# Every second gate and up block with four pairs of k-tiles in seven products, every down block of four strips with three, low parts in one piece, and small inputs later

## The chip, the cores and the metric

The kernel runs on one core of one Trainium2 chip. The metric is the device time of one execution in microseconds (us); the times given are medians of several runs. The core has a matrix engine (TensorE, in the profile PE for its matmuls and PEld for its weight loads), a vector engine (VectorE, DVE), a scalar engine (ScalarE, ACT), a general engine (GpSimd, POOL) and a queue engine (SyncE, SP) that here only issues DMAs. Each engine works through its own instructions in a fixed order and waits on semaphores for the others.

## The reference

Two layers of a decoder over 256 positions and 2048 features, in float32. What the change touches most is the feed-forward network (FFN) at the end of each layer:

```python
def swiglu(x, w_gate, w_up, w_down):
    return (jax.nn.silu(x @ w_gate) * (x @ w_up)) @ w_down
...
for layer in range(DEPTH):
    xn = rms_norm(x, norm_mix[layer])
    if layer % 2 == 0:
        x = x + mixer_mlstm_ssd(xn, *mixer_params[layer])
    else:
        x = x + mixer_moba(xn, *mixer_params[layer])
    x = x + swiglu(rms_norm(x, norm_ffn[layer]), *ffn_params[layer])
return rms_norm(x, final_norm)
```

`w_gate` and `w_up` are 2048 x 5632, `w_down` is 5632 x 2048. The mixer of layer 0 begins with a projection `xn @ w_in`, whose first columns are the queries of an mLSTM; its gates, a decay table and masks come from small inputs (`ssd_a_log`, `mlstm_gate_bias`, convolution weights and the like).

## The kernel before

**Matmuls in two parts.** A float32 operand is split into a high part of type fp32r (`wh`, `xh`: a copy by ACT) and the rest (`wl`, `xl`: source minus high part, by DVE). One product of a 128x128 tile of activations with 512 weight columns is then three matmuls that accumulate in PSUM: high by high, high by low, low by high (`add`, L473).

**Pairs of k-tiles.** `block` (L458) computes 256 positions by 1024 output columns (two strips of 512) over `nk` k-tiles, two k-tiles at a time. For each pair `weights` (L429) loads 2 x 512 KB of weights into `raw`, ACT writes `wh`, DVE writes `wl`. A **plain pair** ("P" in a plan) is 2 position halves x 2 strips x 2 k-tiles = 8 products, 24 matmuls. A **seven-product pair** ("S") follows Strassen's scheme: DVE forms four sums of weights from `raw` (L450, L451, L453) and needs four sums of activations (`sums_of`, `activation_sums`, kept in tiles `skx` or `skh`), both are split again, and 7 products, 21 matmuls, do. Its weight tiles come in two units: `wl<-raw` with 1536 elements (three parts) and `wl<-sums` with 2 x 1024. Products 2, 3, 4 go into the block's accumulators (`acc_f`, PSUM banks 0 to 3), products 1, 7, 5, 6 into `acc_e`, banks 4 to 7. When the last S pair is done, four additions by DVE make `pre` from `acc_e` (L521 to L525); when the last pair is done, two more, L1008 (or L909 for a down block), add `acc_f` to it. `acc_f` has one set of banks, so the next block's first matmul waits for the first of these two.

**Plans.** A plan says which kind comes at each position: `PLAN_X = "PSPSPSPP"` for gate and up blocks, `PLAN_LATE = "PPPSPSPP"` for the first of a network, `PLAN_H` for down blocks.

**The FFN** (`ffn`, L1001) goes through 11 strips of 512 hidden features in groups of 4, 4 and 3. `hidden` makes one strip: a block with the gate columns as one strip and the up columns as the other, then silu and product (`h`), a copy by a DMA of POOL's queue into `hr` (type fp32r), and eight transposes on PE into `p_tr` (banks 6, 7, 4, 5 in turn) that are split into `ha` or `hb`. They are put off by `later(wait, ...)`; while a block has S pairs left, `held` stops the clock of these waits. After a group, `add_blocks` runs two down blocks over its strips, the first for output columns 0 to 1023, the second for the others. I number strips 0 to 10 and call the two down blocks of a group its **first** and **second down block**.

**Buffers.** `raw` has three buffers and a spare that serves every fourth use; `wh` and `wl` have three each (`unit`, L122). A plain pair takes one of each, an S pair two. A buffer of `wh` is free when PE's last matmul with it is done.

**Order.** A scheduler places the instructions of each engine by priorities (`high_priority`) and by its own idea of when operands are ready, so the order on an engine, PE included, can differ from that of the code.

**The beginning.** PE runs eleven idle matmuls (`keep_busy`), while `first_x`, the first weights and small inputs are loaded: `alog`, `ident_in`, `pv`, `d_bc`, `gbias`, `mask_sl` on POOL's queue, `cw_rows` on ACT's. `chunks` (L352) brings the weights of a strip in pieces of two k-tiles, `input_ready` splits the input's k-tiles beside them.

## Time and profile before

| | |
|---|---|
| median of 3 runs | 2559.82 us (2558.21 to 2562.22) |
| the profiled execution | 2558.07 us, of which 2556.3 us are the span of its instructions |
| busy PE, DVE, ACT | 99%, 85%, 57% of the span |
| granted PE clock | 0.999 |
| FFN of layer 0 | blocks start at 769.65 us, end at 1469.77 us |
| FFN of layer 1 | blocks start at 1849.01 us |

The page gives one execution: busy time of each engine, the chain of work that ended last, and the costliest groups of instructions, each named by source line, engine, operation and tile, with idle time in front of them and who ended it. A matmul's row shows its start and about 0.39 us; the next one starts well before that has passed, so the distance from start to start is the one to count with.

### The profile page before, as it was taken

Reading aid. Unit: us, or ns where it says so; the run is one execution under the profiler, and the core shown is the slowest. Engines: PE = TensorE matmul, PEld = TensorE weight load, DVE = VectorE, ACT = ScalarE, POOL = GpSimd, SP = SyncE. Lnnn points to the kernel's source line nnn. Section 1 sums busy time; section 2 is a strip of 40 time slices with the busy share of each in tenths; the row PEclk is TensorE's granted clock in tenths of the full one; section 3 lists DMA queues with packets and bytes.
Section 4 is the critical chain, followed back from the end, with each engine's and each line's share of the span. In section 5 each row is a group of like instructions: output and inputs, shape, how many; then the busy total and the mean of one; then the engine's idle time right before and its main releaser. Section 6 shows DMA issues by size and latency. Waiting matters only on the chain.

```text
span 2556.3 us, 32504 instructions
## 1 busy us (share of the span) xinstructions
PE 2541.2 (99%) x12179; PEld 2129.6 (83%) x12179; DVE 2176.5 (85%) x2679; ACT 1465.2 (57%) x1940; POOL 59.7 (2%) x112
## 2 busy tenths in 40 slices
PE   9999999999999999999999999999999999999998
PEld 8888888888888888888888888888888888888887
DVE  5776778798989998999899987767999988998898
ACT  6465665566556554555455655666665545564554
POOL 1000010000000000000000000000000000000000
PEclk9999999999999999999999999999999999999999
DMA  8665576566565666566656556554556756575754
GB/s 281 181 209 185 165 231 185 167 204 214 181 214 182 217 212 202 200 222 216 196 200 212 196 172 230 165 165 149 196 184 213 234 177 222 198 239 167 236 190 165
DMA packets 257774, 509.58 MB, mean 199 GB/s; under 512 B 16232, under 2 KB 16512, under 8 KB 257104
## 3 DMA queue, kind: packets, MB, share of 16 engines
q1 hardware_dynamic: 249952, 483.20, 58.0%
q0 software_dynamic: 6224, 21.56, 2.4%
q10 hardware_dynamic: 1440, 2.75, 0.3%
q8 instruction: 95, 1.56, 0.2%
q14 instruction: 63, 0.52, 0.1%
HBM read 494.76 MB, written 2.14 MB: 194 GB/s over the span
## 4 chain that ended last, share of the span: by engine, by line
PE 94%; DVE 3%; issue 1%; DMA 1%; ACT 1%; SPq 0%; POOLq 0%; POOL 0%; DVEq 0%; ACTq 0%
PE acc_f L475 19%; PE acc_f L476 18%; PE acc_f L477 18%; PE acc_w L383 11%; PE acc_w L387 6%; PE acc_e L475 4%; PE acc_e L477 4%; PE acc_e L476 4%; PE acc_a L413 2%; PE acc_a L414 2%; PE acc_a L415 2%; PE p_y L872 1%; PE p_tr L284 1%; DVE wl L443 1%; DMA raw<-in_l_w_o 1%
## 5 line engine op out<-in xcount | busy, mean ns | idle before, releaser
L441 ACT CAST wh<-raw 128x1024 fp32r<-128x1024 f32 (+1 forms) x573 | 628.6, 1137 | 496.7 <-PE acc_f L477 384.1
L443 DVE TENSOR_TENSOR wl<-raw,wh 128x1024 fp32r<-128x1024 f32 (+1 forms) x573 | 745.8, 1327 | 119.2 <-ACT wh L441 115.8
L475 PE MATMUL acc_f<-wh,x 128*128 128x512 f32 x1122 | 438.6, 391 | 0.5 <-DVE xres L909 0.5
L477 PE MATMUL acc_f<-wh,x 128*128 128x512 f32 x1122 | 436.9, 389 | 0.0
L476 PE MATMUL acc_f<-wl,x 128*128 128x512 f32 x1122 | 436.6, 389 | 0.0
L368 DVE TENSOR_TENSOR wl<-raw,wh 128x1024 fp32r<-128x1024 f32 (+1 forms) x225 | 271.0, 1217 | 130.5 <-ACT wh L367 126.8
L441 ACT CAST wh<-sums 128x1024 fp32r<-128x1024 f32 x230 | 234.8, 1051 | 199.7 <-PE acc_f L477 137.4
L367 ACT CAST wh<-raw 128x1024 fp32r<-128x1024 f32 (+1 forms) x225 | 231.7, 1044 | 184.4 <-PE acc_w L383 94.4
L443 DVE TENSOR_TENSOR wl<-sums,wh 128x1024 fp32r<-128x1024 f32 x230 | 273.6, 1219 | 11.9 <-ACT wh L441 11.7
L477 PEld LDWEIGHTS acc_f<-wh,x 128*128 128x128 f32 x1122 | 210.6, 188 | 44.1
L475 PEld LDWEIGHTS acc_f<-wh,x 128*128 128x128 f32 x1122 | 210.6, 188 | 43.8 <-issue 0.9
L476 PEld LDWEIGHTS acc_f<-wl,x 128*128 128x128 f32 x1122 | 210.6, 188 | 43.0
L383 PE MATMUL acc_w<-xa,wh 128*128 128x512 f32 x768 | 207.9, 398 | 2.9 <-ACT wh L367 1.9
L383 PEld LDWEIGHTS acc_w<-xa,wh 128*128 128x128 f32 x768 | 139.2, 189 | 29.1 <-ACT wh L367 3.3
L450 DVE TENSOR_TENSOR sums<-raw 128x1024 f32<-128x1024 f32 x115 | 140.2, 1219 | 23.0 <-DMA raw<-in_l_ffn_up 11.3
L383 PE MATMUL acc_w<-x,wh 128*128 128x512 f32 x512 | 139.2, 399 | 0.0
L387 PE MATMUL acc_w<-xa,wl 128*128 128x256 f32 x768 | 121.1, 282 | 0.0
L387 PEld LDWEIGHTS acc_w<-xa,wl 128*128 128x128 f32 x768 | 109.6, 190 | 6.5
L383 PEld LDWEIGHTS acc_w<-x,wh 128*128 128x128 f32 x512 | 92.4, 189 | 16.9
L475 PE MATMUL acc_f<-wh,hb 128*128 128x512 f32 (+1 forms) x272 | 105.1, 387 | 0.0
L477 PE MATMUL acc_f<-wh,hb 128*128 128x512 f32 (+1 forms) x272 | 105.1, 386 | 0.0
L476 PE MATMUL acc_f<-wl,hb 128*128 128x512 f32 (+1 forms) x272 | 105.1, 386 | 0.0
(354 smaller groups left out, 4567.9 us busy)
## 6 DMA issues: line engine op xcount, KB each, us to landing
raw<-in_l_w_in SPq DMA_DIRECT2D x191, 512.0 KB, 3.7
raw<-in_l_ffn_gate SPq DMA_DIRECT2D x176, 512.0 KB, 3.9
raw<-in_l_ffn_up SPq DMA_DIRECT2D x176, 512.0 KB, 4.8
raw<-in_l_ffn_down SPq DMA_DIRECT2D x176, 512.0 KB, 5.1
raw<-in_l_w_qkv SPq DMA_DIRECT2D x96, 512.0 KB, 4.6
raw<-in_l_w_out SPq DMA_DIRECT2D x64, 512.0 KB, 5.1
raw<-in_l_w_o SPq DMA_DIRECT2D x32, 512.0 KB, 4.7
hr<-h POOLq DMA_DIRECT2D x40, 256.0 KB, 4.0
```

The lines of the kernel that those rows point to most:

```text
L367: nc.scalar.copy(wh[:, ks, :], raw[:, ks, :])
L368: nc.vector.tensor_sub(wl[:, ks, :], raw[:, ks, :], wh[:, ks, :].bitcast(F32))
L383: return nc.tensor.matmul(banks[f], wh[:, kk, f * P:(f + 1) * P], kt.both(k0 + kk), start=k0 + kk == 0, stop=False, skip_group_check=True)
L387: nc.tensor.matmul(banks[f][:, :T], wl[:, kk, f * P:(f + 1) * P], kt.parts(k0 + kk)[0], start=False, stop=k0 + kk == nk - 1, skip_group_ch ...
L413: nc.tensor.matmul(banks[t], xh[:, ts], wh[:, kk, :], start=k0 + kk == 0, stop=False)
L414: nc.tensor.matmul(banks[t], xh[:, ts], wl[:, kk, :], start=False, stop=False)
L441: nc.scalar.copy(h[:, c, :], of[:, c, :])
L443: nc.vector.tensor_sub(l[:, c, :], of[:, c, :], h[:, c, :].bitcast(F32))
L450: nc.vector.tensor_sub(sums[:, 0:2, :], raw[:, 2:4, :], raw[:, 3:0:-2, :])
L475: nc.tensor.matmul(dst, ah, bh, start=start, stop=False)
L476: nc.tensor.matmul(dst, ah, bl, start=False, stop=False)
L477: nc.tensor.matmul(dst, al, bh, start=False, stop=stop)
```

## The change

Four parts:

1. **More S pairs in the FFN.** Strips 1, 3, 5, 7 and 9 use `PLAN_X4 = "PSPSSPSP"`, with pairs 1, 3, 5, 7 in seven products; the sums of pair 7's activations are made in the first such strip of each group and thrown away before the down blocks. The first down block of a group of four has `"PSPSPSPP"` in place of `"PSPSPPPP"`. The last strip of every group, not only of the last group, is transposed without the copy through POOL's queue and one position earlier.
2. **Whole low parts.** In the FFN the low part of a plain pair, and that of the sums, is one subtraction of 2048 elements in place of two of 1024. The two copies of ACT stay.
3. **Small inputs later.** The small loads move behind those of `xin`, all on POOL's queue, and their consumers behind the second query strip; `keep_busy` has 10 matmuls; the first two k-tiles of input and weights alternate on ACT.
4. **Gate columns and masks later.** The transposes that make `cols` are put off by four ticks, and the addition of the mask to decay rows by two.

```diff
+PLAN_X4 = "PSPSSPSP"
-PLAN_H = {4: ("PSPSPPPP", "PSPSPSPP"), 3: ("PSPSPP", "PSPSPP")}
+PLAN_H = {4: ("PSPSPSPP", "PSPSPSPP"), 3: ("PSPSPP", "PSPSPP")}
...
-    keep_busy(11)
+    keep_busy(10)
...
-    nc.gpsimd.dma_start(alog[32:64], col1(a["l0_ssd_a_log"]))
...
+            if k == 0 and lead is not None:
+                for i, eng in enumerate((nc.scalar, nc.sync)):
+                    eng.dma_start(raw[:, i, :], rows[:, i, :])
+                with tc.high_priority(offset=2000):
+                    for i in range(KC):
+                        with tc.issue_after(cast.ins) if i else nullcontext():
+                            xh, xl = lead(i)
+                        with tc.issue_after(xh.ins):
+                            cast = nc.scalar.copy(wh[:, i, :], raw[:, i, :])
...
-            for c in cuts:
+            for c in (slice(0, cuts[-1].stop),) if whole_lows[0] else cuts:
                 nc.vector.tensor_sub(l[:, c, :], of[:, c, :], h[:, c, :].bitcast(F32))
...
+    xin_loads = [nc.gpsimd.dma_start(xin[t], x_in[t * P:(t + 1) * P, :]) for t in range(NT)]
...
+    with tc.issue_after(xin_loads[0].ins):
+        nc.gpsimd.dma_start(cw_rows, a["conv_w_columns"])
+        nc.gpsimd.dma_start(pv, a["columns"])
+        nc.gpsimd.dma_start(alog[32:64], col1(a["l0_ssd_a_log"]))
+        nc.gpsimd.dma_start(ident_in, a["ident"])
...
+    def turn_cols():
+        pc = aux_bank("p_cols")
...
+    later(4, "cols", turn_cols)
...
+            later(2, ("hm", s), masked, mrows[0])
...
-            _, pre, both, joined = block(((wg_, s * STRIP), (wu_, s * STRIP)), xt, 0, KD, plan)
+            more = plan == PLAN_X4
+            _, pre, both, joined = block(((wg_, s * STRIP), (wu_, s * STRIP)), xt, 0, KD, plan, pairs=(1, 3, 5, 7) if more else None,
+                                         ahead=((3, sums_of, xt, 7, False),) if more and 7 not in xt.sums else ())
...
-            hT.sums = summed(PLAN_H[n][0])
+            hT.sums = {1: None, 3: None}
             for i in range(n):
-                hidden(hT, i, first + i, PLAN_X if first + i else PLAN_LATE, n == 4 or i < n - 1)
+                hidden(hT, i, first + i, PLAN_X4 if i % 2 else PLAN_X if first + i else PLAN_LATE, i < n - 1)
+            del xt.sums[7]
...
-                       ahead=(((5, sums_of, hT, 5, False),) if n == 4 else (), ()))
+                       ahead=(((2, sums_of, hT, 5, False),) if n == 4 else (), ()))
```

The change moves instructions on DVE and PE. The first place is DVE at the end of strip 3: from the low part of the strip's last plain pair to the addition of its accumulators (`pre<-pre,acc_f`). `wl<-raw` with 128x1024 or 128x2048 is the low part of a plain pair, `pre<-pre,acc_e` the additions after the last S pair, `sums` the weight sums of the next block. Before:

```order
L443 TENSOR_TENSOR wl<-raw,wh 128x1024 x3
L522 TENSOR_TENSOR pre<-pre,acc_e 128x512
L443 TENSOR_TENSOR wl<-raw,wh 128x1024
L523 TENSOR_TENSOR pre<-pre,acc_e 128x512
L443 TENSOR_TENSOR wl<-raw,wh 128x1024
L525 TENSOR_TENSOR pre<-pre,acc_e 128x2x512
L443 TENSOR_TENSOR wl<-raw,wh 128x1024
L450 TENSOR_TENSOR sums<-raw 128x1024
L443 TENSOR_TENSOR wl<-raw,wh 128x1536
L451 TENSOR_TENSOR sums<-raw,sums 128x512
L1008 TENSOR_TENSOR pre<-pre,acc_f 128x1024
```

And now, at the end of the same strip:

```order
L449 TENSOR_TENSOR wl<-raw,wh 128x2048
L528 TENSOR_TENSOR pre<-pre,acc_e 128x512
L449 TENSOR_TENSOR wl<-raw,wh 128x2048
L529 TENSOR_TENSOR pre<-pre,acc_e 128x512
L456 TENSOR_TENSOR sums<-raw 128x1024
L531 TENSOR_TENSOR pre<-pre,acc_e 128x2x512
L457 TENSOR_TENSOR sums<-raw,sums 128x512
L1031 TENSOR_TENSOR pre<-pre,acc_f 128x1024 x2
```

Before, the list begins with the first of two plain pairs behind the last S pair; now only one plain pair is left there, and between its low part and the first addition of `acc_f` stand six instructions.

The second place is DVE in the group's first down block, around its second S pair. Here `wl<-raw` 128x2048 belongs to the plain pair behind that S pair, 128x1536 to the third S pair, and the first `wl<-sums` to the second. Before (where this S pair is the last), from the plain pair ahead of it:

```order
L443 TENSOR_TENSOR wl<-raw,wh 128x1024 x2
L453 TENSOR_TENSOR sums<-raw,sums 128x512
L443 TENSOR_TENSOR wl<-raw,wh 128x1536
L1012 SCALAR_TENSOR_TENSOR h<-pre,r_6982,h 128x512
L443 TENSOR_TENSOR wl<-sums,wh 128x1024 x2
```

Now, from the sums of the third S pair:

```order
L456 TENSOR_TENSOR sums<-raw 128x1024
L220 TENSOR_TENSOR ha_8339<-p_tr,ha_8339 128x2x256
L457 TENSOR_TENSOR sums<-raw,sums 128x512
L220 TENSOR_TENSOR ha_8339<-p_tr,ha_8339 128x2x256
L449 TENSOR_TENSOR wl<-raw,wh 128x2048
L449 TENSOR_TENSOR wl<-raw,wh 128x1536
L449 TENSOR_TENSOR wl<-sums,wh 128x2048
```

The low part of the second S pair's sums has moved behind the low parts of the two pairs that follow it in the plan.

The third place is PE at that point. Before, where the second S pair (`ha_7935`, and `skh` for its sums of activations) begins, the three kinds of matmul follow one another in turn (L475 high by high, L476, L477), pair after pair:

```order
L477 MATMUL acc_f<-wh,ha_7935 128x512
L475 MATMUL acc_f<-wh,skh 128x512
L476 MATMUL acc_f<-wl,skh 128x512
L477 MATMUL acc_f<-wh,skh 128x512
L475 MATMUL acc_e<-wh,ha_7935 128x512
L476 MATMUL acc_e<-wl,ha_7935 128x512
L477 MATMUL acc_e<-wh,ha_7935 128x512
```

Now, at the same S pair (here `ha_7926`; `ha_8282` belongs to the plain pair and the S pair behind it):

```order
L483 MATMUL acc_e<-wh,ha_7926 128x512
L481 MATMUL acc_f<-wh,ha_8282 128x512
L481 MATMUL acc_e<-wh,skh 128x512
L482 MATMUL acc_e<-wl,skh 128x512
L483 MATMUL acc_e<-wh,skh 128x512
L481 MATMUL acc_e<-wh,ha_8282 128x512
L482 MATMUL acc_f<-wl,ha_8282 128x512
L481 MATMUL acc_e<-wh,skh 128x512 x2
L483 MATMUL acc_f<-wh,ha_8282 128x512
L481 MATMUL acc_f<-wh,ha_8282 128x512
L481 MATMUL acc_e<-wh,skh 128x512
```

Matmuls of four pairs are mixed there: the last products of the first S pair (the triple of `acc_e<-wh,skh`, `wl`, `wh`), and then half of the following plain pair and four matmuls of the third S pair stand ahead of those that read the second S pair's low sums.

More of the change, by code (lines that the diff above doesn't have):

```diff
@@ L1 @@
-from contextlib import ExitStack
+from contextlib import ExitStack, nullcontext
 import numpy as np
@@ L350, in row_norm, with chunks @@
         return r, rb
-    def chunks(w, col, nk, first=KC):
+    def chunks(w, col, nk, lead=None):
         n = 4 if staging else KC
@@ L359, in chunks @@
                 wl = unit("wl", [P, n, STRIP], "wl", F32R)
-            step = KC if k else first
-            for i in range(0, KC, step):
-                ks = slice(k % n + i, k % n + i + step)
-                eng = nc.scalar if step < KC and i == 0 else nc.sync
-                eng.dma_start(raw[:, ks, :],
-                              w[(k + i) * P:(k + i + step) * P, col:col + STRIP].rearrange("(a p) f -> p a f", p=P))
+            rows = w[k * P:(k + KC) * P, col:col + STRIP].rearrange("(a p) f -> p a f", p=P)
+            ks = slice(k % n, k % n + KC)
+            if k == 0 and lead is not None:
[7 more added lines that the diff above has]
+                            cast = nc.scalar.copy(wh[:, i, :], raw[:, i, :])
+                with tc.high_priority(offset=800), tc.issue_after(xl.ins):
+                    for i in range(KC):
+                        nc.vector.tensor_sub(wl[:, i, :], raw[:, i, :], wh[:, i, :].bitcast(F32))
+            else:
+                nc.sync.dma_start(raw[:, ks, :], rows)
                 with tc.high_priority(offset=800):
@@ L464, in block @@
         n = nk // 2
-        pairs = pairs[:plan.count("S")] if pairs else [j for j in range(n) if plan[j] == "S"]
+        pairs = list(pairs[:plan.count("S")]) if pairs else [j for j in range(n) if plan[j] == "S"]
         rest = [j for j in range(n) if j not in pairs]
@@ L606, in hybrid_trunk @@
     lam = cst.tile([64, 1], F32, name="lam")
-    with tc.issue_after(emptied[0].ins):
-        nc.scalar.activation(lam, alog, AF.Exp)
-    with tc.issue_after(emptied[1].ins):
-        nc.vector.tensor_scalar(lam, lam, -1.0, None, op0=OP.mult)
     for dst, c0, s in ((qT, C_Q, 1), (kT, C_K, 0), (kT, C_K, 1)):
@@ L617, in hybrid_trunk @@
                 emptied = lin_sum(banks[f], qT[:, 4 + f, :])
+            with tc.issue_after(emptied[1].ins):
+                nc.vector.tensor_scalar(convw, cw_rows, 0.5, None, op0=OP.mult)
+                nc.vector.tensor_scalar(convb, pv[:, G_CB:G_CB + 32], 0.5, None, op0=OP.mult)
+            with tc.issue_after(emptied[0].ins):
+                nc.scalar.activation(lam, alog, AF.Exp)
+            with tc.issue_after(emptied[1].ins):
+                nc.vector.tensor_scalar(lam, lam, -1.0, None, op0=OP.mult)
             continue
@@ L687, in hybrid_trunk @@
     nc.gpsimd.dma_start(scr[MH:MH + SH], cum[32:64])
-    pc = aux_bank("p_cols")
-    for t in range(NT):
-        nc.tensor.transpose(pc[:, t * P:(t + 1) * P], colsrc[:, t * P:(t + 1) * P], ident)
     cols = held_tile("cols", [P, NT, P], "cols")
     ncols = held_tile("cols", [P, NT, P], "ncols")
-    nc.vector.tensor_copy(cols, pc[:, :T].rearrange("p (a b) -> p a b", a=NT))
-    nc.vector.tensor_scalar(ncols, cols, -1.0, None, op0=OP.mult)
+    def turn_cols():
+        pc = aux_bank("p_cols")
+        for t in range(NT):
+            nc.tensor.transpose(pc[:, t * P:(t + 1) * P], colsrc[:, t * P:(t + 1) * P], ident)
+        nc.vector.tensor_copy(cols, pc[:, :T].rearrange("p (a b) -> p a b", a=NT))
+        nc.vector.tensor_scalar(ncols, cols, -1.0, None, op0=OP.mult)
+    later(4, "cols", turn_cols)
     CU, CCS, CDT, CEM = 0, 32, 64, 96
```

58 lines of the change are left out of this document (27 added, 31 removed).

## The prediction

> **What bounds the kernel now.** I read the page first, then PE's waits, then the timeline of single blocks, and last the busy time block by block. The page:
>
> ```profile
> PE 2541.2 (99%) x12179; PEld 2129.6 (83%) x12179; DVE 2176.5 (85%) x2679; ACT 1465.2 (57%) x1940; POOL 59.7 (2%) x112
> PE 94%; DVE 3%; issue 1%; DMA 1%; ACT 1%; SPq 0%; POOLq 0%; POOL 0%; DVEq 0%; ACTq 0%
> ```
>
> PE is 94% of the chain that ended last; nearly all of the rest is the beginning and the end. What PE waited for in the whole execution:
>
> ```profile
> PE acc_w L383 <- ACT wh L367: 1.9, 1, 1.9
> PE p_idle L186 <- POOL alog L203: 1.0, 1, 1.0
> PE acc_w L383 <- DVE xa L227: 1.0, 1, 1.0
> PE acc_f L475 <- DVE xres L909: 0.5, 1, 0.5
> PE p_cols L690 <- ACT colsrc L681: 0.4, 1, 0.4
> ```
>
> Both `acc_w` waits belong to the first 12 us. So every matmul that goes should shorten the kernel, **as long as DVE, at 85%, stays ahead.** What a matmul is worth is its distance to the next:
>
> ```profile
> 899.67 0.39 PE L476 MATMUL acc_f<-wl,x 128*128 128x512 f32 x1
> ...
> 902.39 0.39 PE L476 MATMUL acc_f<-wl,x 128*128 128x512 f32 x1
> ```
>
> Between these starts lie 12 matmuls: 2.72 / 12 = 0.227 us each, so 5.44 us for a plain pair (24) and 4.76 us for an S pair (21). Now strips 3 and 5 with the blocks behind them (columns: stretch, length, then busy time with counts of PE, PEld, DVE, ACT, POOL, clock, DMA share, GB/s):
>
> ```profile
> 898.09:940.32 42.23, 42.23 (x192) 35.00 (x191) 39.20 (x43) 24.44 (x26) 1.08 (x2) 1.00 0.63 211
> 940.32:983.24 42.92, 42.92 (x195) 35.52 (x194) 37.76 (x42) 21.27 (x23) 1.08 (x2) 1.00 0.64 209
> 1066.20:1108.43 42.23, 42.23 (x192) 35.00 (x191) 37.60 (x37) 23.07 (x24) 1.08 (x2) 1.00 0.63 212
> 1108.43:1150.63 42.20, 42.20 (x193) 35.00 (x191) 39.15 (x43) 24.31 (x26) 1.08 (x2) 1.00 0.63 212
> ```
>
> PE has no gap, and each length is its matmuls (183 or 186 x 0.227) plus eight transposes. DVE is busy for 93, 88, 89 and 93%.
>
> **What goes.** Five strips in each of two FFNs and two first down blocks in each: 14 pairs become S pairs, 14 x 3 x 0.227 = **-9.5 us** on PE.
>
> **What DVE pays.** Its back-to-back rows give the cost from start to start:
>
> ```profile
> 901.69 1.22 DVE L450 TENSOR_TENSOR sums<-raw 128x1024 f32<-128x1024 f32 x1
> 902.83 0.68 DVE L224 TENSOR_TENSOR ha<-xg,ha 128x512 fp32r<-128x512 f32 x1
> 903.43 0.68 DVE L451 TENSOR_TENSOR sums<-raw,sums 128x512 f32<-128x512 f32 x1
> ...
> 907.11 0.28 DVE L315 TENSOR_TENSOR sf<-xg 128x128 f32<-128x128 f32 x1
> 907.31 0.28 DVE L316 TENSOR_TENSOR sf<-sf,xg 128x128 f32<-128x128 f32 x1
> 907.51 0.74 DVE L1012 SCALAR_TENSOR_TENSOR h<-pre,r,h 128x512 f32<-128x512 f32 x1
> 908.18 1.75 DVE L443 TENSOR_TENSOR wl<-raw,wh 128x1536 fp32r<-128x1536 f32 x1
> 909.84 0.28 DVE L317 TENSOR_TENSOR sf<-xg,sf 128x128 f32<-128x128 f32 x1
> ```
>
> That is 1.13 for 1024 elements, 0.60 for 512, 0.20 for 128, 0.67 for the product that makes `h`, 1.67 for 1536. The line through them gives 2.20 for 2048, which the trace does not show; a merge then saves 2 x 1.13 - 2.20 = 0.07 us. An S pair costs 1.13 + 0.60 + 0.60 + 1.67 + 2.20 = 6.20 against 2.20 for a plain one, so +4.0 us on DVE for -0.68 us on PE. Strip 3 goes to 39.20 + 4.0 - 8 x 0.07 = 42.7 us of DVE in 41.5 us of PE; its down block to 41.2 in 42.2. Strip 5, which also makes the sums of pair 7 (0.60 + 4 x 0.20 + 0.60 = 2.0), goes to 43.1 in 41.5. **DVE becomes the bound of these blocks**, and buffers allow a lead of two pairs at most.
>
> **Where PE will wait, first place: the end of a strip with four S pairs.** The nearest row is the one block whose plan already ends in "SP", the last down block of layer 0:
>
> ```profile
> 1466.15 1.22 DVE L443 TENSOR_TENSOR wl<-raw,wh 128x1024 fp32r<-128x1024 f32 x1
> 1467.29 1.21 DVE L525 TENSOR_TENSOR pre<-pre,acc_e 128x1024 f32<-128x1024 f32 x1
> 1468.42 2.34 DVE L909 TENSOR_TENSOR xres<-xres,acc_f 128x1024 f32<-128x1024 f32 x2
> ...
> 1468.84 0.39 PE L477 MATMUL acc_f<-wh,ha 128*128 128x512 f32 x1
> ...
> 1469.77 0.47 PE L475 MATMUL acc_f<-wh,x 128*128 128x512 f32 x1 [0.55 <-DVE xres L909]
> ```
>
> PE began the next block 0.93 - 0.23 = 0.70 us late, because the first addition of `acc_f` came too late on DVE. In the new order the same tail has two weight sums more ahead of that addition. Count from the start S of the last S pair on PE. The buffer of the last plain pair is freed then; ACT makes two copies, which take
>
> ```profile
> 924.17 2.00 ACT L441 CAST wh<-raw 128x1024 fp32r<-128x1024 f32 x2 [1.50 <-PE acc_f L477]
> ```
>
> 2.0 us, and with the semaphores on both sides DVE begins the low part, now in one piece, at S + 2.3. Then come 2.20 (it), 0.60, 2.20 (next block), 0.60, 1.13, 1.13, 0.60 and the addition, which ends after 1.21: S + 11.97. PE needs 4.76 + 5.44 + 0.64 for eight transposes = S + 10.84. PE is late by 1.13, and 0.14 for the semaphore (1468.42 + 1.21 to 1469.77). The scheduler put two matmuls of the next S pair into the hole, 0.45, which leaves **0.8 us** per strip, where 0.68 was won. Strips 1, 5 and 9 in two FFNs: 6 x 0.8 = **+4.8**. Bounds: 0, if DVE takes its additions earlier, and 1.3, if the two hoisted matmuls wait for their own copy.
>
> **Second place: the first down block of a group of four** (4 of them). The same count runs on. From S + 2.3 to the end of the low sums of the block's second S pair DVE has, by the new order, six pieces of 2048 (13.2), three of 1536 (5.0), six of 1024 (6.8), twelve of 512 (7.2), two `h` (1.3) and three of 128 (0.6): 34.1 us without a wait for anything, so S + 36.4, and 0.2 until PE sees it. PE has ahead of the matmul that reads them 10.84 us, then 24 + 21 + 24 + 9 + 12 + 4 + 4 = 98 matmuls (22.2) and eight transposes of the uncopied strip (0.8): S + 33.8. The difference, **2.8 us**, is lost at this strip's end and in the down block together: 4 x 2.8 = **+11.2**. Bounds: 0.8 (only the end of the strip counts, and the block's two last plain pairs give DVE the time back) and 4 (PE also waits for copies that ACT makes in the mixed order).
>
> **Smaller terms.** In strips 3 and 7 the low sums of the second of two neighbouring S pairs end on DVE about 0.25 us after PE needs them by the same count: 4 x 0.25 = +1.0 (0 to 1 each). Merging also makes the first product of a plain pair wait for the second copy; one row of timeline shows that a pair behind an S pair has 4.76 us for 2.3 + 2.2, so it just fits: +0.5 in all (0 to 5, since ACT's copies come later where a DMA is late). Four strips are transposed in float32 instead of fp32r:
>
> ```profile
> 934.13 0.80 PE L282 MATMUL p_tr<-ident_r,hr 128*128 128x128 f32 x8
> 934.77 0.46 PE L475 MATMUL acc_f<-wh,x 128*128 128x512 f32 x1
> ...
> 1441.08 1.03 PE L284 MATMUL p_tr<-ident_r,xres 128*128 128x128 f32 x8
> 1441.87 0.48 PE L475 MATMUL acc_f<-wh,ha 128*128 128x512 f32 x1
> ```
>
> 0.79 against 0.64 us, 4 x 0.15 = +0.6. At the beginning PE's second piece waits for weights, and ACT for their landing:
>
> ```profile
> 9.92 1.04 ACT L367 CAST wh<-raw 128x1024 fp32r<-128x1024 f32 x1 [1.95 <-DMA raw<-in_l_w_in]
> 11.02 2.12 PE L383 MATMUL acc_w<-xa,wh 128*128 128x512 f32 x8 [1.91 <-ACT wh L367]
> ```
>
> Without the small loads beside them these weights land earlier, and the first copy no longer stands behind two splits of the input: between 0 and the two waits of 1.9 and 1.0 together; I take -1.2. The wait for `p_cols` goes: -0.5. Masks and gate columns are read two and more ticks later than they are now made, under matmuls; if that cover fails, one more wait of the kind of 0.4 us comes back. The loads of `xt` pair 7's sums take no DMA, and the DMA share of 0.6 leaves room for the same bytes.
>
> **The sum.** -9.5 - 1.2 - 0.5 + 0.6 + 4.8 + 11.2 + 1.0 + 0.5 = **+6.9 us** on the profiled execution's 2558.07: 2565.0. The median shown lies 1.75 above that execution, so I forecast **2566.7** as the median.
>
> **A rule against the rows.** Rows of one instruction say 1219 ns for 1024 elements and 1753 ns for 1536:
>
> ```profile
> L443 DVE TENSOR_TENSOR wl<-raw,wh 128x1024 fp32r<-128x1024 f32 x458 | 546.5, 1219 | 103.2 <-ACT wh L441 100.4
> L443 DVE TENSOR_TENSOR wl<-raw,wh 128x1536 fp32r<-128x1536 f32 x115 | 201.6, 1753 | 16.0 <-ACT wh L441 15.4
> ```
>
> By them 2048 elements take 2287 ns, and if neighbours did not overlap, a merge would save 2 x 1219 - 2287 = 151 ns, not 67. The Trainium skill, "VectorE: DVE Perf Modes", section on the TRN2 errata, says so: the fixed part is paid between instructions, a large tile pays once. The trace's starts, 1.13 apart for rows of 1.22, speak against the full saving. As a rival it takes 0.08 us from each merged low part: two in a strip's tail, six in the down block's count, so 6 x 0.64 + 4 x 2.3 + the rest: 2563.7.
>
> **Rivals.**
> - *Only the strips' ends wait.* The two plain pairs at the end of the down block, and matmuls in another order, cover its chain: ten times 0.8 = 8.0 in place of 17.0 with the small terms, so -9.5 - 1.2 - 0.5 + 0.6 + 8.0 = -2.6: 2557. For it: the end-of-block row above cost PE only 0.7 us. Against it: 34 us of DVE work stand in one row without a plain pair's slack between.
> - *DVE keeps up everywhere*, so that PE keeps all: -9.5 - 1.2 - 0.5 + 0.6 = -10.6: 2549. For it: the FFN as a whole needs DVE for some 95% only. Against it: the end-of-block row above.
> - *The mixed order binds.* PE waits in order for copies and low parts of the hoisted matmuls in nearly every FFN block, 0.4 us in each of 22 strips and 0.7 more in each of the four down blocks: +11.6: 2578. It decides once ACT's copy, not DVE, is last in front of a hoisted matmul.
>
> **Chances.** Forecast 0.50 (its own range 2562 to 2572), merging saves more 0.05, only the ends 0.22, DVE keeps up 0.15, mixed order 0.08. A measurement can tell about 0.2%, 5 us, from no change. Slower by more (over 2564.9): 0.38 of the forecast, 0.08 and 0.02, so 0.48; within: 0.12 + 0.17 + 0.03 = 0.32; faster (below 2554.7): 0.15 + 0.05 = 0.20. The range 2550 to 2576 leaves out about half of "keeps up" and half of "mixed order".
>
> **What would show it.** Right: a wait of PE's first `acc_f` matmul for DVE's L1031 in ten strips or in the blocks behind them; a down block of 45 us where it was 42.9, with PE waiting for `wl<-sums`; DVE at 96% and more over strips 3 to 4. Wrong: first down blocks of 42.3 us, or strips with four S pairs followed by the next block without a gap. The beginning shows in the start of PE's second group, 11.02 us before.

## The result, and the profile after

| | before | after |
|---|---|---|
| median | 2560.03 us (2558.21 to 2562.22) | 2595.58 us (2593.96 to 2598.11) |
| ratio | | 1.014, 95% interval 1.0128 to 1.0152 |
| span of the profiled execution | 2556.3 us | 2592.2 us |

The kernel is 1.4% slower, 36 us. The direction was forecast; the size was not: the measured median lies 29 us above the forecast of 2566.7 and 20 us above the upper end of its range, 2576. The page after the change has (busy time, share, count; then the chain):

```profile
PE 2557.7 (99%) x12135; PEld 2121.0 (82%) x12135; DVE 2223.1 (86%) x2507; ACT 1490.7 (58%) x1960; POOL 56.2 (2%) x105
PE 86%; DVE 6%; issue 3%; DMA 3%; ACT 2%; SPq 0%; DVEq 0%; POOLq 0%; POOL 0%; ACTq 0%
```

44 matmuls fewer (the 42 of the 14 new S pairs, 2 idle ones), and yet the page counts PE as busy for 16.5 us more. Busy time therefore hides the loss here: rows of matmuls behind a wait are drawn longer than the usual 0.39 us (0.50 at 940.57, below). The chain tells more: PE's share of it falls from 94 to 86%. What PE waited for in the whole execution:

```profile
PE acc_f L482 <- DVE wl L449: 10.0, 12, 4.6
PE acc_e L481 <- ACT wh L447: 6.0, 17, 1.3
PE p_tr L279 <- DVE xres L930: 2.9, 2, 2.5
...
PE acc_f L481 <- DVE pre L1031: 0.7, 4, 0.2
PE p_cols L707 <- ACT colsrc L694: 0.4, 1, 0.4
```

The columns are the total in us, how many waits, and the longest. The wait that was to be largest, for the addition L1031, is 0.7 us; low parts and copies are 16. The stretches of strip 3, the first down block behind it, strips 5 and 6, the last block of layer 1's mixer and strip 0 of layer 1 (columns as before: length, busy PE, PEld, DVE, ACT, POOL, clock, DMA share, GB/s):

```profile
897.39:939.27 41.88, 41.84 (x189) 34.33 (x188) 39.03 (x35) 24.55 (x25) 1.08 (x2) 1.00 0.60 202
939.27:986.49 47.22, 45.19 (x194) 34.68 (x193) 42.49 (x40) 24.27 (x27) 0.00 (x0) 1.00 0.58 189
1070.25:1111.90 41.65, 41.65 (x189) 34.34 (x188) 39.57 (x37) 24.52 (x25) 1.07 (x2) 1.00 0.62 205
1111.90:1155.02 43.12, 42.91 (x194) 34.98 (x193) 41.82 (x37) 25.47 (x29) 1.07 (x2) 1.00 0.64 217
1816.96:1865.07 48.11, 45.12 (x211) 37.04 (x210) 43.59 (x61) 31.41 (x46) 0.00 (x0) 1.00 0.60 202
1865.07:1915.42 50.35, 45.70 (x195) 37.46 (x193) 40.31 (x39) 24.29 (x34) 1.12 (x1) 0.90 0.50 167
```

The down block went from 42.92 to 47.22 us, but DVE is busy for only 90% of it: it is not out of time, it waits as well. The two last rows were 43.76 and 43.96 before, and the change does not seem to touch the first of them. The block starts of the two traces give the account. "The seam" is the name used below for the last block of layer 1's mixer and strip 0 of layer 1's FFN:

| stretch | after minus before, us |
|---|---|
| start to the first FFN block | -1.2 |
| ten odd strips | -4.2 |
| six strips behind an odd one | +5.3 |
| four first down blocks | +17.7 |
| their second down blocks | +2.9 |
| down blocks of the last groups | +5.2 |
| the seam | +10.7 |
| other blocks | +0.3 |
| behind the last block | -0.9 |

The first row is no more than chance allows: the 19 traces of kernels with the new beginning start their first FFN block anywhere from 767.8 to 770.2 us, and the one trace before starts it at 769.65.

### The profile page after: what moved, and what is told of

Same layout as the page of the kernel before. It is cut to its first block, busy times and chain, and to the rows that moved or that the text cites. A ratio compares the mean times of both kernels' runs of the same rounds, so it can differ in the third digit from the quotient of the medians.

```text
span 2592.2 us, 32355 instructions
## 1 busy us (share of the span) xinstructions
PE 2557.7 (99%) x12135; PEld 2121.0 (82%) x12135; DVE 2223.1 (86%) x2507; ACT 1490.7 (58%) x1960; POOL 56.2 (2%) x105
## 4 chain that ended last, share of the span: by engine, by line
PE 86%; DVE 6%; issue 3%; DMA 3%; ACT 2%; SPq 0%; DVEq 0%; POOLq 0%; POOL 0%; ACTq 0%
PE acc_f L482 16%; PE acc_f L483 16%; PE acc_f L481 16%; PE acc_w L387 11%; PE acc_w L391 6%; PE acc_e L482 4%; PE acc_e L481 4%; PE acc_e L483 4%; DVE wl L449 3%; DMA raw<-in_l_ffn_down 2%; PE acc_a L417 2%; PE acc_a L418 2%; PE acc_a L419 2%; ACT wh L447 1%; DVE xres L930 1%
## 5 line engine op out<-in xcount | busy, mean ns | idle before, releaser
L447 ACT CAST wh<-raw 128x1024 fp32r<-128x1024 f32 (+1 forms) x559 | 619.3, 1150 | 346.6 <-PE acc_f L483 272.1
L449 DVE TENSOR_TENSOR wl<-raw,wh 128x2048 fp32r<-128x2048 f32 (+2 forms) x401 | 721.2, 1814 | 79.0 <-ACT wh L447 71.4
L447 ACT CAST wh<-sums 128x1024 fp32r<-128x1024 f32 x258 | 267.2, 1051 | 332.5 <-DVE sums L459 138.2
L483 PE MATMUL acc_f<-wh,x 128*128 128x512 f32 x1062 | 414.5, 390 | 0.0
L481 PE MATMUL acc_f<-wh,x 128*128 128x512 f32 x1062 | 413.9, 393 | 0.4 <-DVE xres L930 0.3
L373 DVE TENSOR_TENSOR wl<-raw,wh 128x1024 fp32r<-128x1024 f32 x223 | 269.8, 1223 | 128.1 <-ACT wh L372 124.4
L449 DVE TENSOR_TENSOR wl<-sums,wh 128x2048 fp32r<-128x2048 f32 (+1 forms) x152 | 298.2, 1967 | 50.2 <-ACT wh L447 50.0
L372 ACT CAST wh<-raw 128x1024 fp32r<-128x1024 f32 x223 | 230.6, 1048 | 183.2 <-PE acc_w L387 95.3
L482 PEld LDWEIGHTS acc_f<-wl,x 128*128 128x128 f32 x1062 | 199.9, 188 | 48.3 <-DVE wl L449 6.8
L481 PEld LDWEIGHTS acc_f<-wh,x 128*128 128x128 f32 x1062 | 199.9, 188 | 43.9 <-DVE pre L1031 1.7
L483 PEld LDWEIGHTS acc_f<-wh,x 128*128 128x128 f32 x1062 | 199.9, 188 | 41.0
L482 PE MATMUL acc_f<-wl,ha 128*128 128x512 f32 x256 | 101.0, 395 | 2.4 <-DVE wl L449 2.0
L482 PE MATMUL acc_e<-wl,skx 128*128 128x512 f32 x261 | 102.2, 391 | 0.4 <-DVE wl L449 0.3
```

Source lines behind the costliest of these rows:

```text
L372: nc.scalar.copy(wh[:, ks, :], raw[:, ks, :])
L373: nc.vector.tensor_sub(wl[:, ks, :], raw[:, ks, :], wh[:, ks, :].bitcast(F32))
L447: nc.scalar.copy(h[:, c, :], of[:, c, :])
L449: nc.vector.tensor_sub(l[:, c, :], of[:, c, :], h[:, c, :].bitcast(F32))
L481: nc.tensor.matmul(dst, ah, bh, start=start, stop=False)
L482: nc.tensor.matmul(dst, ah, bl, start=False, stop=False)
```

## The experiments

Unless another kernel is named, each is the changed kernel with the edit shown. "Start alone" below is the run `e4_start_only`, 2556.6 us. A cost in a block is its length against that of the kernel before.

### The four parts, one by one

**Halves.**

```diff
-        whole_lows[0] = True
+        whole_lows[0] = False
```

> The changed kernel with the low parts of the FFN in halves again (two of 1024 elements); more S pairs, uncopied last strips and the late small inputs stay. Theory A (the merge is the loss: a low part that needs both copies ends later in the scheduler's plan, the matmuls are mixed, and at the change from mixer to FFN of layer 1 DVE puts it behind the residual additions): the 10.7 us at that seam and the 5.2 us in the last group's down blocks go, the first down blocks lose about 2 instead of 4.3 to 4.9: 2595.6 - 10.7 - 5.2 - 4 x 2.5 = about 2570 or less. Theory B (DVE is simply out of time around the third S pair and behind strips with four): the first down blocks stay at 47 us, only the seam goes: about 2583.

Measured: 2575.76 us, 1.0065 (1.005 to 1.008). Halves give 19.8 us back, 11 of them in the last groups' down blocks (5.0), the second down blocks (2.9), and the strips behind an odd one (0.5 each). The first down blocks stay at 46.5 to 46.8 and the seam at +7.5, so neither theory holds alone: the seam was to go under both.

**Old first down blocks.**

```diff
-PLAN_H = {4: ("PSPSPSPP", "PSPSPSPP"), 3: ("PSPSPP", "PSPSPP")}
+PLAN_H = {4: ("PSPSPPPP", "PSPSPSPP"), 3: ("PSPSPP", "PSPSPP")}
...
-                       ahead=(((2, sums_of, hT, 5, False),) if n == 4 else (), ()))
+                       ahead=(((5, sums_of, hT, 5, False),) if n == 4 else (), ()))
```

> The changed kernel with the first down blocks of groups of four as before (two S pairs, sums of the third pair's activations at the old place); whole low parts and the strips with four S pairs stay. Theory B: the four first down blocks go from 47.0 to 47.7 back to 42.9 and the second ones from 42.0 to 42.5 back to 41.5: 2595.6 - 4 x 5.2 = about 2575. Theory A (mixed order of the merged low parts is the loss): they stay above 45 in spite of the fourth plain pair: about 2588. The seam between mixer and FFN of layer 1 keeps its 10.7 us under both.

Measured: 2581.12 us, 1.0085 (1.007 to 1.01). The first down blocks take 45.6: two S pairs as before, and still 2.7 us more than before. The seam did not keep its 10.7 us, as both theories had it, but fell to 3.1, and 7.7 of the 14.5 us gained are there.

**Three S pairs in all strips.**

```diff
-                hidden(hT, i, first + i, PLAN_X4 if i % 2 else PLAN_X if first + i else PLAN_LATE, i < n - 1)
+                hidden(hT, i, first + i, PLAN_X if first + i else PLAN_LATE, i < n - 1)
-            del xt.sums[7]
+            xt.sums.pop(7, None)
```

> The changed kernel with three S pairs in every strip; whole low parts and three S pairs in all down blocks stay. Theory C (the tail of a strip with four S pairs starts the DVE backlog that the first down block pays, as the forecast counted): odd strips 42.2, the strips behind them 42.2 instead of 43.1, first down blocks about 43 to 44 instead of 47: 2595.6 - 4 x 3.5 - 2 = about 2580. If the first down block's loss is its own: they stay at 46 to 47 and the time at about 2593.

Measured: 2579.13 us, 1.0079 (1.0064 to 1.0094). The first down blocks are 43.7 to 43.9: their loss comes for the most part from the strip with four S pairs ahead of them. Odd strips, with the old plan but whole low parts, lose up to 1.6 each. The seam costs 4.1 here.

**Start alone**: the three edits above and the old rule for copied strips (`n == 4 or i < n - 1`) together.

> The kernel before with nothing but the late small inputs, the alternating first weights and the late gate columns and masks. The forecast has -1.2 - 0.5 for these: 2558.3 against 2560.0. The changed kernel's FFN of layer 0 begins 1.2 us earlier, which says 2558.8. A rival: the late gate columns and masks cost time elsewhere in the mixer (then 2560 or more).

Measured: 2556.61 us, 0.9992 (0.9983 to 1.0002): 2.5 us by the medians, but the interval does not exclude no gain at all; its first product block starts 1.8 us earlier in the trace.

### The seam

```diff
     open_stage("g", FFN)
+    turn["spare"] = -1
```

> The changed kernel, with the counter that hands every fourth load to the spare raw buffer restarted before the FFN of layer 1. In the kernel before, 240 loads had been counted there (240 mod 4 = 0, the spare comes fourth); the change adds 5 + 2 loads in the FFN of layer 0, so the spare comes first and the first weights of strip 0 wait for memory that the attention part still uses. Theory D (this phase is the loss at the seam): the 10.7 us in the last block of the mixer and strip 0 go, 2595.6 - 10.7 = 2585; if the merged low parts hold 3.2 of it (after minus halves), 2588. Rival (the merge alone puts the low part late there): 2595, no change.

Measured: 2586.14 us, 1.0105 (1.009 to 1.012), 9.4 us less than the changed kernel. The seam's two blocks in that run:

```profile
1817.85:1861.93 44.08, 43.53 (x200) 36.05 (x200) 40.84 (x46) 27.67 (x37) 0.00 (x0) 1.00 0.65 210
1861.93:1907.54 45.61, 44.37 (x204) 36.22 (x202) 42.40 (x54) 27.84 (x42) 1.12 (x1) 1.00 0.55 193
```

Against 43.76 and 43.96 before, 8.8 of the 10.7 us go; with halves as well (all later runs with this restart and halves) the seam is within 0.5 us of before. **The phase of the spare buffer is the cause of most of the seam's loss.** Runs with whole low parts in which the counter stands at another phase agree: 3.1 and 4.1 us are lost there in the runs with the old down blocks (5 loads more than before) and with the old strips (2 more), against 10.7 with 7 more. The way is not the one expected: in the changed kernel the first weights are issued 16 us ahead of the place where strip 0 should begin, as before (1832.62 for 1849.01).

```profile
1844.09 0.37 SPq L440 DMA_DIRECT2D raw<-in_l_ffn_gate  x1
```

But PE's order there is another. Transposes of `xres` stand ahead of strip 0 and between its first matmuls, and these and the low part of the first pair wait for DVE:

```profile
1862.94 0.41 PE L279 MATMUL p_tr<-ident_r,xres 128*128 128x128 f32 x2 [2.51 <-DVE xres L930]
...
1872.21 0.80 PE L482 MATMUL acc_f<-wl,x 128*128 128x512 f32 x1 [4.64 <-DVE wl L449]
1872.81 0.63 PE L483 MATMUL acc_f<-wh,x 128*128 128x512 f32 x1
1873.23 0.63 PE L481 MATMUL acc_f<-wh,x 128*128 128x512 f32 x1
```

How the buffer's phase makes the scheduler choose that order I did not follow.

### The order on PE

Written order for the FFN (each matmul kept behind the one traced before it, with the restart of the spare):

```diff
-            nc.tensor.matmul(dst, ah, bh, start=start, stop=False)
+            kept(nc.tensor.matmul(dst, ah, bh, start=start, stop=False))
```

> As the run with the restarted counter, and in the FFN PE's matmuls are kept in the order in which the code writes them. Theory M (merged low parts cost because the scheduler then mixes the matmuls of neighbouring pairs, and PE waits in order for copies of the later pair): the FFN goes to what it takes with halves, 16 us less than the restarted counter alone, about 2569. Theory L (the low part itself is late, since it starts only behind the second copy): no gain, 2585 or more. A mixture lies between.

Measured: 2636.53 us, 1.0303 (1.0287 to 1.0318), 50 us worse than with the restart of the spare alone. Then with the products alone in a chain, transposes free:

```diff
+        def queued(*args, **kw):
+            with tc.issue_after(last_mm[0].ins) if last_mm[0] is not None else nullcontext():
+                last = nc.tensor.matmul(*args, **kw)
+            last_mm[0] = last if in_ffn[0] else None
...
-            nc.tensor.matmul(dst, ah, bh, start=start, stop=False)
+            queued(dst, ah, bh, start=start, stop=False)
```

> As the changed kernel with the spare's counter restarted (2586), and the products of the FFN are issued on PE in the order of the code, while transposes stay free to move (in the run with everything in written order PE stood 34 us at transposes). If mixing is what makes merged low parts dear, 2570; if mixing is the scheduler's way round a low part that is late, each plain pair of an FFN block that was mixed waits for both copies and the low part instead: 2586 to 2600.

Measured: 2649.28 us, 1.0349 (1.0333 to 1.0364), 63 us worse. The waits of PE in both (the first row is of the written order, the second of the chain of products):

```profile
PE p_tr L279 <- DVE h L1038: 33.8, 6, 5.8
```

```profile
PE p_tr L279 <- DVE h L1041: 30.2, 7, 5.4
```

**Mixing covers waits; without it they cost more.** In order, PE stands some 5 us at the uncopied strip's transposes in each group. Not all of the 50 and 63 us are such waits: the granted clock is 0.990 and 0.986 over these two runs, against 0.997 in the changed kernel. By these shares up to some 24 and 34 us may be lost to half clock (an estimate: the missing share of the clock times the span, less the 3 us or so that every run has at its end). So the price of the written order by itself is not known, only that it is no gain. The waits pointed to the next question: who needs these transposes so soon?

### Why the first down block loses 4 us

The new runs of this part have halves and the restarted spare. Four S pairs only in the second strip of a group:

```diff
-                hidden(hT, i, first + i, PLAN_X4 if i % 2 else PLAN_X if first + i else PLAN_LATE, i < n - 1)
+                hidden(hT, i, first + i, PLAN_X4 if i == 1 else PLAN_X if first + i else PLAN_LATE, i < n - 1)
```

> Low parts in halves, the spare's counter restarted, four S pairs only in the second strip of each group (never right ahead of a down block), three S pairs in all down blocks. If the loss of the first down block comes from the tail of the strip ahead of it, the down block takes about 42.5 and each second strip saves 0.39 with the one behind it: 2556.6 (start alone) - 6 x 0.4 - 4 x 0.4 = about 2552.5. If the third S pair of the down block costs by itself 3 us, 2566.

Measured: **2552.86 us**, 0.9975 (0.9966 to 0.9985), the fastest of all runs. First down blocks 42.64 to 42.69.

Three S pairs in every strip (`PLAN_X` for all):

> Low parts in halves, the spare's counter restarted, three S pairs in every strip, three S pairs in all down blocks. The third S pair alone: if DVE has the time, 2556.6 - 4 x 0.68 + 4 x 0.15 = 2554.5; if it brings a wait of its own as with whole low parts (+0.8 to 1.0 in each first down block, 0.3 to 0.8 in the second), 2560.

Measured: 2555.46 us, 0.9987 (0.9977 to 0.9996). The third S pair of a first down block is worth 0.2 us there.

Four S pairs with the tail moved:

```diff
-PLAN_X4 = "PSPSSPSP"
+PLAN_X4 = "PSSPSSPP"
```

> As the run before it without the priority of h, and the plan with four S pairs is PSSPSSPP, so that two plain pairs stand behind the last S pair again. Theory C (the tail): first down blocks 42.7, strips behind odd ones 42.2, odd strips 41.5: 2555.5 - 10 x 0.68 = 2548.7. Rival: two neighbouring S pairs ask 12.4 us of DVE in 9.5 us of PE, and four units of weights at once: 1 to 2 us lost in each odd strip, 2560 to 2570.

Measured: 2598.71 us, 1.015 (1.0135 to 1.0166). The theory of the tail, which the run with four S pairs in one strip had seemed to bear out, is not borne out here: strips 3 and 7 take 40.80, their matmuls and nothing else, but the down block behind them takes 50.1 to 51.1. Strips 1, 5 and 9, which also make pair 7's sums, lose 2.2 to 3.0. It is no clean test, though, since the plan also puts two S pairs side by side. What these down blocks lose is lost at their start, where the changed kernel lost about 1 us: PE waits for DVE's additions of the strip ahead, the transposes of strips 2 and 6 run there, and for 6.8 us in each of them PE has half clock (0.50 in the second view).

```profile
PE acc_f L481 <- DVE pre L1031: 6.6, 4, 1.8
```

```profile
944.70:951.50 6.80, 5.03 (x14) 4.03 (x15) 6.80 (x10) 2.03 (x3) 0.00 (x0) 0.50 0.48 154
```

And `h` earlier:

```diff
-                nc.scalar.activation(h, g, AF.Silu, scale=r[:, t:t + 1])
-                nc.vector.scalar_tensor_tensor(h, u, r[:, t:t + 1], h, op0=OP.mult, op1=OP.mult)
+                with tc.high_priority(offset=1600):
+                    nc.scalar.activation(h, g, AF.Silu, scale=r[:, t:t + 1])
+                    nc.vector.scalar_tensor_tensor(h, u, r[:, t:t + 1], h, op0=OP.mult, op1=OP.mult)
```

> Low parts in halves, the spare's counter restarted, four S pairs in every odd strip and three in all down blocks (2575.8 - 7.5 = 2568 by the runs so far), and silu and the product that makes h have the priority of the additions ahead of them. If the first down block loses because h of the strip ahead is late on DVE, so that its transposes hold PSUM banks 6 and 7 and the first S pair's products 5 and 6 wait: first down blocks 43 to 44 in place of 46.7, 2568 - 4 x 3 = 2556. If DVE's backlog itself is the loss: 2568, since the same work is only in another order.

Measured: 2570.64 us, 1.0044 (1.0027 to 1.0061), first down blocks 46.7 to 48.3: no gain. The trace of the run with halves shows why. Its timeline around the first S pair of the first down block (start, length, engine and instruction, idle time in front):

```profile
954.23 0.87 PE L279 MATMUL p_tr<-ident_r,h 128*128 128x128 f32 x6
...
959.07 0.39 PE L481 MATMUL acc_e<-wh,skh 128*128 128x512 f32 x1
...
962.47 0.47 PE L481 MATMUL acc_e<-wh,skh 128*128 128x512 f32 x1
...
964.54 0.73 PE L481 MATMUL acc_e<-wh,skh 128*128 128x512 f32 x2 [1.13 <-ACT wh L447]
```

```profile
958.17 0.68 DVE L220 TENSOR_TENSOR ha<-p_tr,ha 128x512 fp32r<-128x512 f32 x1
...
961.64 0.68 DVE L220 TENSOR_TENSOR ha<-p_tr,ha 128x512 fp32r<-128x512 f32 x1
```

```profile
963.45 2.00 ACT L447 CAST wh<-sums 128x1024 fp32r<-128x1024 f32 x2 [0.43 <-PE acc_e L483]
```

The matmuls at 959.07 and 962.47 are, by their tile names in the program, products 5 and 6 of the **first** S pair, 13 and 17 us behind its product 3 (945.76). They write PSUM banks 6 and 7, and these hold the transposes of the strip just finished until DVE has split them: each product starts about 0.2 us after the end of its bank's split (958.85, 962.32). The next copy of sums by ACT, for the second S pair, goes into the `wh` buffer that product 6 reads last; it starts at 963.45, and PE waits for it at 964.54. In the run with `h` early the second split still ended at 963.2, since splits had no priority. **So the first down block has a chain that runs over two PSUM banks**, and DVE is in it only because the split is late in its order. In the changed kernel itself one row shows the bank at work: a product of the first S pair waits for DVE's split of `ha`, which ends at 958.70. It reads `wh` and `skh`, so the bank is what it shares with that split.

```profile
958.75 0.50 PE L481 MATMUL acc_e<-wh,skh 128*128 128x512 f32 x1 [0.23 <-DVE ha L220]
```

How much this chain weighs can be read from PE's distances from start to start above 0.227 us. With halves the four first down blocks have 4.3 to 4.5 us of such excess, of which some 3.4 lie 15 to 30 us into the block, at these products and the copies behind them, and 0.7 at its first matmuls. In the changed kernel they have 4.8 to 5.5: 1.0 at the first matmuls, which is the tail of the strip ahead, 1.1 at a whole low part 11 us into the block, about 2 at the banks and the copies behind them, and the rest at later low parts. Two runs test the banks. Two plain pairs in front, still three S pairs:

```diff
-PLAN_H = {4: ("PSPSPSPP", "PSPSPSPP"), 3: ("PSPSPP", "PSPSPP")}
+PLAN_H = {4: ("PPSPSSPP", "PSPSPSPP"), 3: ("PSPSPP", "PSPSPP")}
```

> Low parts in halves, the spare's counter restarted, four S pairs in every odd strip, and the first down block of a group of four runs PPSPSSPP: still three S pairs, but two plain pairs ahead of the first. Theory K (PSUM banks): the transposes of the strip just finished use banks 6 and 7, the first S pair's products 5 and 6 need the same banks and wait until DVE has split the transposed h; the next S pair's sums wait for the buffers of those products. With a plain pair more in front the transposes are through before products 5 and 6: first down blocks 42.5 to 43 in place of 46.7, 2568 - 4 x 4 = about 2552. Theory B (DVE's backlog behind a strip with four S pairs is the loss, wherever it falls): the same DVE work in the same block, 46 and more, 2566 or more.

Measured: 2554.34 us, 0.9979 (0.997 to 0.9988). The first down block of layer 0's first group, with the same S pairs and hardly a gap on PE:

```profile
938.96:981.74 42.78, 42.78 (x191) 35.00 (x192) 40.87 (x46) 22.18 (x25) 0.00 (x0) 1.00 0.57 185
```

Strip 3 ahead of it takes 42.53 where it took 41.78 with halves, so some 0.75 of the nearly 4 us gained in the down block is lost again there. And the old place of the pairs, with early `h` and, shown here, early splits:

```diff
-        with tc.high_priority(offset=1200 if kt.name in ("x1", "x2", "x3") else 0):
+        with tc.high_priority(offset=1200 if kt.name in ("x1", "x2", "x3") or src[0].dtype != F32R and kt.name[0] == "h" else 0):
```

> As the run with early h (2570.6), and the splits of the transposed h of an uncopied strip have a priority above weights too. Theory K: the run with early h did not gain because banks 6 and 7 were still held until DVE's second split at 962.5, 24 us into the block; with the splits early the products 5 and 6 come earlier and the first down blocks take 43 to 44.5: 2556 to 2560. Theory B: 2570.

Measured: 2559.55 us, 0.9999 (0.999 to 1.0009), 11 us less than with early `h` alone; first down blocks 44.5 to 45.4, the second split ends at 956.9 (956.21 + 0.68) in place of 963.2. Both runs speak for the banks and against the backlog as the main part. They don't settle all of it: two plain pairs in front also give DVE more time ahead of the first S pair, and with early splits 1.6 to 2.5 us of the loss stay, at least 0.7 of them where PE waits for low parts some 31 us into the block, so that DVE's time does count there:

```profile
PE acc_f L482 <- DVE wl L449: 1.9, 4, 0.8
```

### What the merge costs

Start alone, plus whole low parts:

> The kernel before with the late small inputs (2556.6 by itself) and the whole low parts in the FFN, nothing else: plans, copied strips and the phase of the spare buffer are those of before. The forecast gave the merge +0.5 with a bound of 5: 2557 to 2562. From the runs so far (changed kernel minus halves 19.8, of which 3.2 at the seam) the merge should cost 10 to 17 even where DVE has time to spare: 2567 to 2574, in the last group's down blocks and in every block that follows a plain pair.

Measured: 2575.24 us, 1.006 (1.0045 to 1.0075): 18.6 us by itself. Then for sums alone, and (with `is raw`) for plain pairs alone:

```diff
-            for c in (slice(0, cuts[-1].stop),) if whole_lows[0] else cuts:
+            for c in (slice(0, cuts[-1].stop),) if whole_lows[0] and of is not raw else cuts:
```

> The kernel before with the late small inputs, and whole low parts for the sums of S pairs alone (plain pairs in halves). Theory L (a merged low part costs because it starts behind the second copy and ends as a whole, and PE needs the first half of a plain pair's at once): sums have nine products ahead of them and lose little, 2556 to 2560. Rival (merging as such, by the order that the scheduler makes of it): half of the 18.6 that both together cost, about 2566.

> The same with whole low parts for plain pairs alone. Theory L: nearly all of the 18.6, so 2572 to 2576. Rival: about 2566.

Measured: 2559.79 us, 1.0001 (0.9992 to 1.001), and 2569.01 us, 1.0036 (1.0023 to 1.0049): 3.2 for sums (little more than the noise of two medians), 12.4 for plain pairs, 3.0 more when both are merged. The larger part is the plain pairs', as the theory of lateness said, but 2569 lies between its forecast of 2572 to 2576 and the rival's 2566. One place in the run with both shows it, in strip 1, where a load came late:

```profile
835.30 3.95 DVE L449 TENSOR_TENSOR wl<-raw,wh 128x2048 fp32r<-128x2048 f32 x2
```

```profile
837.64 0.50 PE L482 MATMUL acc_f<-wl,x 128*128 128x512 f32 x1 [0.89 <-DVE wl L449]
```

PE's matmul reads only the first half of that low part. In halves, at the 1.22 of a row of 1024 elements, it would by this estimate have been ready at 836.5, before PE stopped at 836.75; merged, the first of the two instructions ends at 837.6.

### The strip's tail

Two plain pairs first, as above, and in every block the first S pair's products kept behind the plain pair ahead of them:

```diff
-            nc.tensor.matmul(dst, ah, bh, start=start, stop=False)
+            with tc.issue_after(behind[0].ins) if behind[0] is not None else nullcontext():
+                nc.tensor.matmul(dst, ah, bh, start=start, stop=False)
...
+                behind[0] = newest[0] if i_ == first_s else None
                 for p in (2, 3, 1, 7, 5, 6, 4):
```

> As the run with two plain pairs first (2554.3), and the products of a block's first S pair are queued on PE behind the last product of the plain pair ahead of them. In that run one product of the first S pair stands ahead of the block's first plain pair and waits 0.93 us (1.07 with the restart of PE) for ACT's copy, in each of the four first down blocks. If this misplaced product is all that strips 3 and 7 lose there: 2554.3 - 4 x 1.1 = 2549.9. If the product only made visible that DVE's addition in front of the block is late, PE waits for that in its place: 2553 to 2554.

The second run adds the early `h` and early splits:

> As the run before it, and h and the splits of the transposed h have priority over weights. PE's order then has almost no mixed pair left in the down blocks. If banks 6 and 7 still cost something in the first down blocks (1.30 over the matmuls in the run with two plain pairs first, of which 0.8 are eight float32 transposes): 2549.9 - 4 x 0.4 = 2548.3. If DVE's time, given to h, is missing at the weights: 2550 to 2553.

Measured: 2556.91 us, 0.9994 (0.9985 to 1.0003), and 2554.72 us, 0.9983 (0.9974 to 0.9992). The misplaced product is gone, and a wait has taken its place, ten times, once behind each odd strip:

```profile
PE acc_f L484 <- DVE pre L1036: 6.0, 10, 1.0
```

That is the second expectation of the first of these runs: the product only filled the hole in front of DVE's late addition. It is slower than that expectation since strips 1, 5 and 9 lose too, 41.90 where they took 41.44: there such a product had filled the hole, at a cost of 0.2 in the strip behind. Neither version beats four S pairs in the second strips alone.

## Why the prediction was wrong

**Right: the DVE count at a strip's end.** It said that DVE begins the last plain pair's low part at S + 2.3 and ends the first addition of `acc_f` at S + 11.97, S being the start of the last S pair on PE. In strip 3 of the changed kernel S is 928.55, and the trace has

```profile
930.82 2.29 DVE L449 TENSOR_TENSOR wl<-raw,wh 128x2048 fp32r<-128x2048 f32 x1 [1.23 <-ACT wh L447]
...
936.43 1.22 DVE L456 TENSOR_TENSOR sums<-raw 128x1024 f32<-128x1024 f32 x1
...
939.30 2.35 DVE L1031 TENSOR_TENSOR pre<-pre,acc_f 128x1024 f32<-128x1024 f32 x2
```

```profile
940.57 0.50 PE L481 MATMUL acc_f<-wh,ha 128*128 128x512 f32 x1 [0.16 <-DVE pre L1031]
```

930.82 is S + 2.27; the addition ends at 939.30 + 1.22 = S + 11.97, and PE starts 0.05 later. A 2048-element low part takes 2.21 from start to start, estimated as 2.20 (930.82 to 933.03). PE is late by 1.18 against the count and fills 0.45 with two matmuls of the next S pair, so 0.7 for a forecast 0.8. The six strips behind strips 1, 5 and 9 lost 5.3 for a forecast 4.8. Ten odd strips and the six behind them together came out at +1.1 with merged low parts; the ten S pairs themselves would have saved 6.8.

**Wrong, the term of 0.5 for the merge** ("a pair behind an S pair has 4.76 us for 2.3 + 2.2, so it just fits"). It costs 18.6 alone, 19.8 in the changed kernel, the largest error of the sum. The step took a lead that holds in a steady strip and let the whole low part stand for PE's demand; where a load, a residual addition or a transpose has eaten the lead, the matmul that needs half of it waits for all of it, behind both copies. The bound of 5 was put for late loads alone. That plain pairs carry 12.4 of the 18.6 was measured; which lead was eaten in each block was followed in the one place shown.

**Wrong, the second place: 2.8 us for a strip's end and its first down block, by DVE's backlog.** The first down blocks lost 4.1 to 4.9, and the strip's end is in that: 1.0 of it. The backlog itself was counted well: the second S pair's low sums were to be ready at S + 36.4, and DVE ended them at 965.96 = S + 37.4. But PE did not stand still for them: from 962.8 to 972.6 its matmuls start 0.23 to 0.25 apart. With halves the loss stays (3.6 to 3.9), and with the same S pairs and the transposes ahead of the first S pair it goes, but for some 0.75 in the strip ahead. What held the block with halves was in the main PSUM banks 6 and 7, between the uncopied strip's transposes and products 5 and 6; in the changed kernel they account for about 2 us and whole low parts for nearly as much. The count of DVE's instructions contained the splits as 0.6 us each, without asking who waited for them. That the last strip of every group is now transposed without the copy stood in the change and in the sum only as 0.6 us of slower transposes. The 1.6 to 2.5 us that early splits leave are not explained beyond the waits for low parts.

**Missing: the seam.** Two blocks that the change seemed not to touch lost 10.7 us. The new plans take seven loads more in layer 0, so the counter that gives every fourth load to the spare buffer stands at 247 instead of 240 when layer 1's FFN begins. The sum had no term for it: its terms were for blocks whose plan or instructions the edits name. The restart of the counter gives 8.8 of the 10.7 back; how the phase makes the order on PE is open.

**The rest.** The beginning: PE's second group starts with no wait now,

```profile
9.25 2.14 PE L387 MATMUL acc_w<-xa,wh 128*128 128x512 f32 x8
```

against 11.02. What of these 1.8 us is left where the FFN begins, 1.2 in this trace, cannot be told from chance; the start alone measured 2.5 us by the medians, with an interval that does not exclude no gain, for a forecast 1.7. The wait for `p_cols`, 0.4, did not go at all. The rival "the mixed order binds", at 2578 and with 0.08 the nearest, is not borne out as a price of mixing: kept in order, PE is 50 us slower still, half clock included. Its sign for deciding, ACT's copy last in front of a hoisted product, was seen 17 times for 6.0 us; four of these, 0.59 each, are the last link of the bank's chain in the first down blocks. With the seam and the merge taken off (the run with halves, less 7.5) the S pairs cost 11.7 us over the start alone; the forecast's terms for them sum to +8.1. That this comes near is partly luck, since the larger of these terms, 11.2, rested on the wrong wait.

## What to carry to other kernels

Where a change makes an operation coarser, ask for each reader how much of it the reader needs first: merges that were to save 0.07 us each cost 18.6 us together, and where it was followed, PE wanted the first half. Follow buffers with two users (here two PSUM banks between transposes and products) as a chain of their own; the engine that appears in the wait may only be the one that happens to free them. And where buffers are dealt out by a running counter, every change of a plan upstream shifts the deal downstream: compare the order at each seam, not only in the blocks that were edited.

## What was not expected of the hardware

At the seam PE's clock fell to half. Around the wait of 4.64 us the granted clock is 0.50, where the six other stretches above have 1.00:

```profile
1864.81:1875.05 10.24, 5.59 (x18) 4.19 (x17) 9.94 (x15) 7.23 (x18) 0.00 (x0) 0.50 0.31 102
```

By the clock's record half clock begins at 1864.81, so it was not this wait that brought it: it had begun before it, 1.9 us after the wait of 2.51 us for `xres` ended. Behind the wait, matmuls of 512 columns started 0.43 us apart (1872.81, 1873.23 and so on), and 0.23 apart again from about 1875. The Trainium skill, "TensorE: Matmul & The Clock Gate", Part 1, says that the clock is halved until PE has been busy for about 3.4 us. The trace roughly agrees: full clock is back at 1875.05, 2.8 us after PE resumed. A long wait costs its own length and here some 1.4 us more (seven matmuls at 0.2). In the run with the tail moved it began at 944.70 behind two waits of 0.44 and 0.58 us (ending at 942.66 and 943.70), so no long wait stood in front of it there.

A short wait costs more than it shows, too: behind the wait of 0.16 us at 940.57 the next matmul starts 0.33 us later (940.90) in place of 0.227, and the same 0.1 us stands behind most waits of PE in these traces. Why was not followed.
